# Two-input SBUF operations moved from GpSimd to VectorE, SBUF copies and 256-channel norms to ScalarE, in a streaming encoder step

## The chip, the cores and the metric

The kernel runs on one core of a Trainium2 chip. The metric is the device time of one launch in microseconds (us). The engines are PE (TensorE, matrix products), DVE (VectorE), ACT (ScalarE), POOL (GpSimd) and SP (SyncE, which issues nearly all transfers). Each takes its instructions strictly in the order of its own list and meets the others only at semaphores.

## The reference, cut to what matters

One encoder layer over 512 prompt tokens and 64 sample tokens of 1024 channels, in float32:

```python
xn = rms_norm(x, g_norm)
hq, hf, hi, za, dq, dk, dv, zb, mq, zm, gr = split_columns(xn @ w_in)   # 13312 columns
y_a = rms_norm(hgrn2_recurrence(...), g_hg_out)       # 8 heads of 128
y_b = rms_norm(diff_softmax(norm(dq), norm(dk), dv)) * (1 - lam_init)   # 8 heads, two maps of 64
y_m = memory_attention(rms_norm(mq, g_mq), mem_k, mem_v)                # 4 heads of 256, 256 memories
h = sum(sigmoid(gr[n]) * ((y_n * silu(z_n)) @ w_branch[n]) for n in range(3))
y = x + h @ w_out
```

`mem_k` and `mem_v` are projections of a normed memory (`w_mkv`); `mem_k` is normed over its 256 channels per head. The sample tokens attend to cached keys and values and carry a recurrent state.

## The kernel before, in words

Precision comes from splitting. Every float32 operand of a large product is held as a rounded high part and a remainder; a product is three matmuls (high by high, high by low, low by high). ACT writes the high part (a copy that rounds, line 214 for weights), DVE or POOL subtracts it from the source to get the low part (line 217).

Work is a list of *jobs*, each for 256 columns of a weight matrix. A job's weights come as two halves (`raw`, three buffers) and are split into *units* of 128x512 (`wh`, `wl`, eight in flight). Jobs are of three kinds. "T" gives channels by tokens (line 332, 296 for its product), "N" gives tokens by channels (line 332 and 345), and "S" is a 2x2 block product with seven instead of eight block products (`strassen`, line 416 on; matmuls on line 459). An S job needs sums of its weight blocks, t1 to t4, made in `plan` by `add` (line 248), and sums of blocks of x, made once in `build_XS` (line 374) and kept in `XS`. Its seven steps of 12 matmuls use four PSUM banks out of a ring of three; evacuations on DVE (lines 424 and 432) free them, so a late one stops PE at a later step or at the next job.

The order of all work is written by the program itself. `run_jobs` walks through the jobs; after every 12 matmuls it makes one *tick* (`weave`): it emits what was put off by `later(n, ...)`, and it advances each running generator by one step. The generators are the attention and recurrence heads; their small matmuls and transposes thus stand between the steps of the jobs. `conv_next` adds one or two weight units per tick. The engines' lists follow this order.

The stages, with their jobs and the generators beside them: the recurrence heads (`hgrn`, jobs of kind T and N); branch 0's output product, beside which `build_XS` runs; the memory's keys and values, the gates `gr` (S); the memory heads (`mem_q_prep`, `mem_kv`, `mem_head`) beside S jobs; the differential heads (`diff_pair`, finished by `finish_heads`) beside N and S jobs; branches 2 and 1 (line 296) with the merge in `branch_jobs`; the output product. `y_splits` (line 654) fetches a branch's outputs again and splits them for the branch product.

POOL has these parts in the stages after the recurrence: every second weight remainder (line 217, by `lo_engine` or by name in `plan`), t3 and t4 (line 248), the remainders of `y_splits` (line 678) and `split_slot` (line 724), half of `build_XS` (line 380), gains in the norms (line 1040), copies between partition halves in `build_k` (line 1113) and `build_s` (1142, 1143), the merge's last add for branch 2 (line 1677), and `rstd`, the power -1/2 on a few columns (lines 140 and 141). In `mem_head`, DVE scales the softmax (line 1518) before PE transposes it (line 1531); in `finish_heads`, DVE scales a head by the softmax's sum (line 739) and by the norm (line 752) before PE transposes it (line 761); in `combine`, DVE joins the two maps (line 1198) before PE transposes them (line 1209).

Of the kernel before, what the change touches and what calls it, by code (L numbers as in the profile page):

```python
# [13 lines left out]
F32 = mybir.dt.float32  # L14
# [7 lines left out]
P = 128  # L22
# [44 lines left out]
def encoder_step(ctx, tc, ins, outs):  # L67
# [101 lines left out]
    def lo_engine():  # L169
        lo_n[0] += 1  # L170
        return ge if lo_n[0] % 2 == 0 else ve
# [28 lines left out]
    def plan(i, j):  # L200
# [38 lines left out]
        else:  # L239
# [11 lines left out]
            def op_t2(now):  # L251
                t1 = add("t1", part(0, 0), part(0, 1), ve)
                t2 = add("t2", sums["t1"], part(1, 1), ve)
                sums["slots"] = t1, t2, add("t3", part(0, 1), part(1, 1), ge)
# [4 lines left out]
            def op_t1(now):  # L259
                t4 = add("t4", sums["t2"], part(1, 0), ge)  # L260
# [5 lines left out]
            ops.append((i, 0, lambda now: split(part(0, 0), P, 0, now, ge)))  # L266
            ops.append((i, 1, op_t2))
            ops.append((i, 1, op_t1))
            ops.append((i, 1, lambda now: split(part(1, 0), P, 1, now, ge)))
            ops.append((i, 1, lambda now: split(sums["t3"], P, None, now, ve, 0, sums["slots"][2])))  # L270
            ops.append((i, 1, lambda now: split(part(1, 1), P, 1, now, ge)))
            ops.append((i, 1, lambda now: split(sums["t4"], P, None, now, ge, 0, sums["t4slot"])))
# [101 lines left out]
    def build_XS():  # L374
# [7 lines left out]
        for k2 in range(2):  # L382
# [5 lines left out]
            tt(ge, t, l22, l21)  # L388
# [3 lines left out]
            tt(ge, s3, h11, h21)  # L392
            ve.scalar_tensor_tensor(out=s2, in0=s1, scalar=-1.0, in1=h11, op0=ALU.mult, op1=ALU.subtract)
            yield
            tt(ge, t, l11, l21)
            tt(ve, s2, s2, l11)
            yield
            tt(ge, s3, s3, t, ALU.add)
# [3 lines left out]
            for n, x in enumerate((s1, s2, s3, s4)):  # L402
# [3 lines left out]
                tt(ge if n % 2 else ve, lo, x, hi.bitcast(F32))  # L406
# [247 lines left out]
    def y_splits(n):  # L654
# [8 lines left out]
        for h in range(8):  # L663
# [14 lines left out]
            ge.tensor_tensor(out=lo[:, 0:TT], in0=tmp[:, 0:TT], in1=hi[:, 0:TT].bitcast(F32), op=ALU.subtract)  # L678
# [37 lines left out]
    def split_slot(x):  # L716
# [6 lines left out]
        def flo():  # L723
            ge.tensor_tensor(out=lo[:, 0:512], in0=x[:, 0:512], in1=hi[:, 0:512].bitcast(F32), op=ALU.subtract)
            slots.put(x)
# [4 lines left out]
    def finish_heads(n, ob, ons, ohp, j, gcol, z, r0=None):  # L730
# [7 lines left out]
        if r0 is not None:  # L738
            ve.tensor_tensor(out=o3, in0=ob.rearrange("p (a b) -> p a b", a=4), in1=r0.unsqueeze(2).to_broadcast([P, 4, P]), op=ALU.mult)
            src = on[:, 0:512]  # L740
            put(ob)
            yield
# [4 lines left out]
        se.activation(out=sq[0:TS, 0:P], in_=ons[0:TS], func=AF.Square, accum_out=ss[0:TS, 4:5])  # L747
        rstd(rs[:, 0:4], ss[:, 0:4], P)
        rstd(rs[0:TS, 4:5], ss[0:TS, 4:5], P)
        for _ in range(4):  # L750
            yield
        ve.tensor_tensor(out=o3, in0=src.rearrange("p (a b) -> p a b", a=4), in1=rs[:, 0:4].unsqueeze(2).to_broadcast([P, 4, P]), op=ALU.mult)
# [259 lines left out]
    def norm_groups(bufs, smp, g, gain=None):  # L1012
# [23 lines left out]
        def apply(x, r):  # L1036
            ve.tensor_tensor(out=grp(x), in0=grp(x), in1=r.unsqueeze(2).to_broadcast([x.shape[0], r.shape[1], g]), op=ALU.mult)
            if gain is not None:
                gb = gain[0 : x.shape[0]].unsqueeze(1).to_broadcast([x.shape[0], r.shape[1], g])
                ge.tensor_tensor(out=grp(x), in0=grp(x), in1=gb, op=ALU.mult)  # L1040
# [3 lines left out]
        if smp is not None:  # L1044
            apply(smp, rs[0:TS, m : m + ns])
            yield
        yield
# [887 lines left out]
```

## Time and profile before

| | us |
|---|---|
| three runs | 1149.35, 1146.55, 1148.5; median 1148.5 |
| the profiled execution, its own time | 1149.15 |
| its span, first to last instruction | 1147.4 |
| PE busy in it | 1098.0 |
| DVE, POOL, ACT busy | 818.0, 612.3, 528.5 |
| mean granted TensorE clock | 0.985 of full speed |

A row of a view by stretches gives, for each engine, busy time and the number of instructions, then the granted TensorE clock (1.00 is full speed), the busy share of the DMA engines and GB/s. A row of waits gives who waited, for whom, the total in us, how often, and the longest. A row of groups gives line, engine, operation, tiles (out<-in), shapes and number, then busy time and the mean of one in ns, then idle time of the engine just before and what ended it. A row of the timeline gives start, duration, engine and operation, and in brackets the idle time before it and what ended that. `slot` stands for any of the general buffers, `d` for a bank of the jobs' products, `abank` for a bank of the heads.

### The profile page before, as it was taken

How to read it: one execution, taken by the hardware profiler on the slowest of the kernel's cores; microseconds unless marked ns; L12 is line 12 of the kernel's file. 1: busy time of each engine (PE TensorE's matmuls, PEld its weight loads, DVE VectorE, ACT ScalarE, POOL GpSimd, SP SyncE). 2: the span in 40 equal slices, each digit the busy share in tenths (PEclk: the TensorE clock that was granted, in tenths of full speed). 3: DMA queues.
4: the chain of work that ended last, by engine and by line, in shares of the span. 5: the costliest groups of instructions: out<-in, count | busy, mean ns of one | idle time of the engine just before them, and what ended most of it. 6: DMA issues, size and time to landing. Idle time of an engine off the chain costs nothing. (4 is left out here: it accounts for less than half of the span.)

```text
span 1147.4 us, 22458 instructions
## 1 busy us (share of the span) xinstructions
PE 1098.0 (96%) x8685; PEld 1079.0 (94%) x8685; DVE 818.0 (71%) x1391; ACT 528.5 (46%) x1227; POOL 612.3 (53%) x682
## 2 busy tenths in 40 slices
PE   8999999998999999989999989998998998999998
PEld 6999999998999999989899989998998998888998
DVE  6479493956637855799895669779869877856532
ACT  6443333233233554646664446645645754543320
POOL 2336444456536876987562564366447485454120
PEclk9999999999999999999999989999999999998999
DMA  5442132234234566634434332223222437555542
GB/s 185 148 152 79 57 105 88 88 102 127 73 111 144 188 221 229 216 128 140 152 116 163 112 108 96 79 88 108 73 81 78 160 123 242 170 181 176 166 133 68
DMA packets 127931, 150.67 MB, mean 131 GB/s; under 512 B 7730, under 2 KB 104654, under 8 KB 127824
## 3 DMA queue, kind: packets, MB, share of 16 engines
q1 hardware_dynamic: 127820, 149.24, 40.5%
q8 instruction: 68, 1.11, 0.4%
q14 instruction: 39, 0.32, 0.1%
q10 hardware_dynamic: 4, 0.00, 0.0%
HBM read 114.74 MB, written 34.47 MB: 130 GB/s over the span
## 5 line engine op out<-in xcount | busy, mean ns | idle before, releaser
L217 POOL TENSOR_TENSOR wl<-raw,wh 128x512 fp32r<-128x512 f32 x172 | 252.7, 1474 | 262.9 <-ACT wh L214 256.1
L332 PE MATMUL d<-wh,xh 128*128 128x256 f32 x768 | 223.4, 291 | 0.7 <-ACT xh L621 0.7
L332 PE MATMUL d<-wh,xl 128*128 128x256 f32 x768 | 218.5, 285 | 1.3 <-DVE xl L624 1.3
L332 PE MATMUL d<-wl,xh 128*128 128x256 f32 x768 | 218.3, 284 | 0.0
L214 ACT ACTIVATE wh<-raw 128x512 fp32r<-128x512 f32 x284 | 167.8, 622 | 4.1 <-DMA raw<-in_w_in_dram 2.2
L296 PE MATMUL d<-slot,wh 128*128 128x288 f32 x768 | 160.1, 303 | 5.1 <-POOL slot L678 5.1
L332 PEld LDWEIGHTS d<-wh,xh 128*128 128x128 f32 x768 | 148.0, 193 | 1.8 <-ACT xh L621 1.1
L332 PEld LDWEIGHTS d<-wh,xl 128*128 128x128 f32 x768 | 147.9, 193 | 1.8 <-DVE xl L624 1.8
L332 PEld LDWEIGHTS d<-wl,xh 128*128 128x128 f32 x768 | 148.2, 193 | 0.4
L217 DVE TENSOR_TENSOR wl<-raw,wh 128x512 fp32r<-128x512 f32 x112 | 116.2, 1040 | 43.7 <-ACT wh L214 42.5
L296 PEld LDWEIGHTS d<-slot,wh 128*128 128x128 f32 x768 | 126.8, 193 | 6.6 <-POOL slot L678 6.2
L459 PE MATMUL d<-XS,wh 128*128 128x288 f32 x640 | 131.5, 299 | 0.0
L296 PE MATMUL d<-xh,wh 128*128 128x288 f32 x384 | 116.8, 304 | 0.0
L296 PE MATMUL d<-slot,wl 128*128 128x288 f32 x384 | 115.2, 300 | 0.0
L296 PE MATMUL d<-xh,wl 128*128 128x288 f32 x384 | 113.1, 295 | 0.0
L296 PE MATMUL d<-xl,wh 128*128 128x288 f32 x384 | 113.1, 295 | 0.0
L459 PEld LDWEIGHTS d<-XS,wh 128*128 128x128 f32 x640 | 103.0, 190 | 0.3
L459 PE MATMUL d<-XS,wl 128*128 128x288 f32 x320 | 94.6, 295 | 0.0
L217 DVE TENSOR_TENSOR wl<-slot,wh 128x512 fp32r<-128x512 f32 x60 | 82.7, 1396 | 12.3 <-ACT wh L214 11.8
L459 PE MATMUL d<-xh,wh 128*128 128x288 f32 x240 | 75.2, 313 | 8.7 <-DVE slot L424 4.4
L459 PE MATMUL d<-xh,wl 128*128 128x288 f32 x240 | 73.1, 305 | 1.9 <-POOL wl L217 1.9
L296 PEld LDWEIGHTS d<-slot,wl 128*128 128x128 f32 x384 | 74.2, 193 | 0.0
(321 smaller groups left out, 2741.5 us busy)
## 6 DMA issues: line engine op xcount, KB each, us to landing
raw<-in_w_in_dram SPq DMA_DIRECT2D x104, 512.0 KB
raw<-in_w_branch_dram SPq DMA_DIRECT2D x24, 512.0 KB
raw<-in_w_mkv_dram SPq DMA_DIRECT2D x16, 512.0 KB
out_dram<-slot SPq DMA_DIRECT2D x31, 256.0 KB
g<-slot SPq DMA_DIRECT2D x24, 288.0 KB
slot<-g SPq DMA_DIRECT2D x24, 288.0 KB
y<-slot SPq DMA_DIRECT2D x20, 288.0 KB
slot<-y SPq DMA_DIRECT2D x20, 288.0 KB
```

The source lines that it names most:

```text
L214: se.activation(out=u.hi, in_=src, func=AF.Copy)
L217: (eng or lo_engine()).tensor_tensor(out=u.lo, in0=src, in1=u.hi.bitcast(F32), op=ALU.subtract)
L296: pe.matmul(out=ps[:, 0:TH], lhsT=w[:, k % 4, :], rhs=x(k)[:, sl], start=(n == 0), stop=(n == 23))
L332: pe.matmul(out=ps[:, t * CW : (t + 1) * CW], lhsT=x(k)[:, sl], rhs=w[:, k % 2, :], start=(n == 0), stop=(n == 23))
L459: pe.matmul(out=ps, lhsT=w[:, k, :], rhs=x(k), start=bool(first and n == 0), stop=stop, skip_group_check=True)
```

## The change

From the moment `XS` exists (that is, from branch 0's output product on), no weight remainder goes to POOL. The sums t3 and t4, `build_XS`, the remainders in `y_splits` (of the first stage as well) and `split_slot`, the gains, and the merge's last add go to DVE. In `build_k` both copies between partition halves go to ACT. The scaling of the softmax in `mem_head` goes to ACT. The norms over 256 channels (memory keys, memory queries) get a function of their own, `norm_256`: one Square per row block with its sum accumulated on ACT, and the scaling on ACT too; the gain is a DVE multiplication one tick later. In `finish_heads`, for the differential heads, the PSUM bank is copied unscaled by ACT, and the softmax's factor is applied to the small columns (its square to the sums, itself to the result of `rstd`). POOL keeps `rstd`, memsets, the small copies in `build_s`, and all that it does in the recurrence stage except `y_splits`.

```diff
     def lo_engine():
         lo_n[0] += 1
-        return ge if lo_n[0] % 2 == 0 else ve
+        return ge if lo_n[0] % 2 == 0 and not XS else ve
...
-                sums["slots"] = t1, t2, add("t3", part(0, 1), part(1, 1), ge)
+                sums["slots"] = t1, t2, add("t3", part(0, 1), part(1, 1), ve)
...
-                t4 = add("t4", sums["t2"], part(1, 0), ge)
+                t4 = add("t4", sums["t2"], part(1, 0), ve)
...
-            ops.append((i, 0, lambda now: split(part(0, 0), P, 0, now, ge)))
+            ops.append((i, 0, lambda now: split(part(0, 0), P, 0, now, ve)))
...
-            ops.append((i, 1, lambda now: split(part(1, 0), P, 1, now, ge)))
+            ops.append((i, 1, lambda now: split(part(1, 0), P, 1, now, ve)))
...
-            ops.append((i, 1, lambda now: split(part(1, 1), P, 1, now, ge)))
-            ops.append((i, 1, lambda now: split(sums["t4"], P, None, now, ge, 0, sums["t4slot"])))
+            ops.append((i, 1, lambda now: split(part(1, 1), P, 1, now, ve)))
+            ops.append((i, 1, lambda now: split(sums["t4"], P, None, now, ve, 0, sums["t4slot"])))
...
             tt(ve, s1, h22, h21)
-            tt(ge, t, l22, l21)
+            tt(ve, t, l22, l21)
...
-                tt(ge if n % 2 else ve, lo, x, hi.bitcast(F32))
+                tt(ve, lo, x, hi.bitcast(F32))
...
-            ge.tensor_tensor(out=lo[:, 0:TT], in0=tmp[:, 0:TT], in1=hi[:, 0:TT].bitcast(F32), op=ALU.subtract)
+            ve.tensor_tensor(out=lo[:, 0:TT], in0=tmp[:, 0:TT], in1=hi[:, 0:TT].bitcast(F32), op=ALU.subtract)
...
         if r0 is not None:
-            ve.tensor_tensor(out=o3, in0=ob.rearrange("p (a b) -> p a b", a=4), in1=r0.unsqueeze(2).to_broadcast([P, 4, P]), op=ALU.mult)
+            se.activation(out=on[:, 0:512], in_=ob, func=AF.Copy)
             src = on[:, 0:512]
+            r2 = small(4, "r2", bufs=3)
+            ve.tensor_tensor(out=r2, in0=r0, in1=r0, op=ALU.mult)
...
+        if r0 is not None:
+            ve.tensor_tensor(out=ss[:, 0:4], in0=ss[:, 0:4], in1=r2, op=ALU.mult)
...
+        if r0 is not None:
+            ve.tensor_tensor(out=rs[:, 0:4], in0=rs[:, 0:4], in1=r0, op=ALU.mult)
...
+    def norm_256(bufs, smp=None, gain=None):
+
+        rows = [(b[:, 256 * t : 256 * t + 256], P) for b in bufs for t in range(2)] + ([(smp, TS)] if smp is not None else [])
...
+        for i, (x, r) in enumerate(rows):
+            se.activation(out=sq[0:r, 0:256], in_=x, func=AF.Square, accum_out=ss[0:r, i : i + 1])
+            if i % 2:
+                yield
...
+        rstd(rs[:, 0:m], ss[:, 0:m], 256)
...
+        for _ in range(4):
+            yield
+        for i, (x, r) in enumerate(rows):
+            se.activation(out=x, in_=x, func=AF.Copy, scale=rs[0:r, i : i + 1])
+            if gain is not None:
+                later(1, lambda x=x: ve.tensor_tensor(out=x, in0=x, in1=gain, op=ALU.mult))
+            if i % 2:
+                yield
...
                 ve.tensor_tensor(out=KL[m][a, 0:T], in0=ps[a], in1=KD[m][a, 0:T].bitcast(F32), op=ALU.subtract)
-                ve.tensor_copy(KD[m][b, 0:T], KD[m][a, 0:T].bitcast(F32))
-                ge.tensor_copy(KL[m][b, 0:T], KL[m][a, 0:T].bitcast(F32))
+                se.activation(out=KD[m][b, 0:T], in_=KD[m][a, 0:T].bitcast(F32), func=AF.Copy)
+                se.activation(out=KL[m][b, 0:T], in_=KL[m][a, 0:T].bitcast(F32), func=AF.Copy)
...
             ve.reciprocal(out=zz[0:R], in_=zz[0:R])
-            ve.tensor_scalar(out=e[0:R, 0:256], in0=e[0:R, 0:256], scalar1=zz[0:R], scalar2=None, op0=ALU.mult)
+            se.activation(out=e[0:R, 0:256], in_=e[0:R, 0:256], func=AF.Copy, scale=zz[0:R])
...
-                (ve if n == 1 else ge).tensor_tensor(out=h2[b][:, sl], in0=h2[b][:, sl], in1=g[:, sl], op=ALU.add)
+                ve.tensor_tensor(out=h2[b][:, sl], in0=h2[b][:, sl], in1=g[:, sl], op=ALU.add)
```

Over the whole program DVE's list grows from 1370 rows to 1578, ACT's from 1084 to 1164, and POOL's shrinks from 685 to 410. Because `norm_256` takes two ticks less than the norm that it replaces for the memory queries, the memory heads' transposes and small products stand up to two ticks earlier between the same matmuls of the jobs, and a few of their transfers stand some rows earlier in SP's list.

The first place is the list of DVE in an S job beside the first memory head, at the end of one job's steps: lines 248 and 217 make t1, t2 and the remainders of the next job, line 424 and 432 evacuate this one. Before:

```order
L424 TENSOR_TENSOR slot_194_4972<-d_6302,slot_194_4972 128x288
L248 TENSOR_TENSOR slot_249_6336<-raw_6168 128x512
L248 TENSOR_TENSOR slot_250_6338<-slot_249_6336,raw_6189 128x512
L217 TENSOR_TENSOR wl_6343<-slot_250_6338,wh_6342 128x512
L217 TENSOR_TENSOR wl_6361<-slot_249_6336,wh_6360 128x512
L424 TENSOR_TENSOR slot_195_4973<-d_6302,slot_194_4972 128x288
L432 SCALAR_TENSOR_TENSOR slot_254_6385<-slot_196_4974,slot_195_4973 128x288
```

The list of POOL for the same stretch holds this before:

```order
L217 TENSOR_TENSOR wl_6296<-slot_238_6184,wh_6295 128x512
L217 TENSOR_TENSOR wl_6316<-raw_6168,wh_6315 128x512
L248 TENSOR_TENSOR slot_251_6340<-raw_6168,raw_6189 128x512
L248 TENSOR_TENSOR slot_252_6358<-slot_250_6338,raw_6189 128x512
L217 TENSOR_TENSOR wl_6382<-raw_6189,wh_6381 128x512
```

DVE's list for the same stretch in the changed kernel (its lines 218, 249, 425 and 433 are lines 217, 248, 424 and 432 of before):

```order
L425 TENSOR_TENSOR slot_194_4973<-d_6307,slot_194_4973 128x288
L218 TENSOR_TENSOR wl_6321<-raw_6176,wh_6320 128x512
L249 TENSOR_TENSOR slot_247_6341<-raw_6176 128x512
L249 TENSOR_TENSOR slot_248_6343<-slot_247_6341,raw_6197 128x512
L249 TENSOR_TENSOR slot_249_6345<-raw_6176,raw_6197 128x512
L249 TENSOR_TENSOR slot_250_6363<-slot_248_6343,raw_6197 128x512
L218 TENSOR_TENSOR wl_6348<-slot_248_6343,wh_6347 128x512
L218 TENSOR_TENSOR wl_6366<-slot_247_6341,wh_6365 128x512
L425 TENSOR_TENSOR slot_195_4974<-d_6307,slot_194_4973 128x288
L433 SCALAR_TENSOR_TENSOR slot_252_6392<-slot_196_4975,slot_195_4974 128x288
```

The two evacuations (line 424 before, 425 now) had four rows of DVE between them, with POOL's rows beside those; now seven rows stand between them, all on DVE, and POOL's list has none of the five.

The second place is ACT's list in `build_k`, at the start of a differential head: line 1091 writes the queries' high parts, 1108 the keys', 439 evacuates a job, 214 splits weights. Before:

```order
L1091 ACTIVATE slot_413_8699<-abank_81,gdq 64x512
L1091 ACTIVATE slot_414_8700<-abank_81,gdq 64x512
L1108 ACTIVATE slot_415_8730<-abank_84 64x512
L1108 ACTIVATE slot_416_8731<-abank_84 64x512
L439 ACTIVATE slot_196_4974<-d_8738 128x288
L214 ACTIVATE wh_8757<-slot_420_8753 128x512
L214 ACTIVATE wh_8796<-slot_419_8751 128x512
```

In the changed kernel (lines 1125, 1142, 440, 215 are the same code, 1146 and 1147 the two copies that DVE and POOL had):

```order
L1142 ACTIVATE slot_407_8734<-abank_84 64x512
L1142 ACTIVATE slot_408_8735<-abank_84 64x512
L440 ACTIVATE slot_196_4975<-d_8742 128x288
L215 ACTIVATE wh_8761<-slot_412_8757 128x512
L215 ACTIVATE wh_8800<-slot_411_8755 128x512
L1146 ACTIVATE slot_407_8734<-slot_407_8734 64x512
L1147 ACTIVATE slot_409_8736<-slot_409_8736 64x512
L1170 ACTIVATE slot_414_8780<-abank_83 64x320
L1171 ACTIVATE slot_414_8780<-abank_83,gdq 64x64
```

Two copies have come into ACT's list; the second (line 1147) reads what DVE's subtraction of the same tick writes, and the first transposed samples (line 1170) and the later weight splits stand behind it.

More of the change, by code (lines that the diff above doesn't have):

```diff
@@ L391, in build_XS @@
             yield
-            tt(ge, s3, h11, h21)
+            tt(ve, s3, h11, h21)
             ve.scalar_tensor_tensor(out=s2, in0=s1, scalar=-1.0, in1=h11, op0=ALU.mult, op1=ALU.subtract)
             yield
-            tt(ge, t, l11, l21)
+            tt(ve, t, l11, l21)
             tt(ve, s2, s2, l11)
             yield
-            tt(ge, s3, s3, t, ALU.add)
+            tt(ve, s3, s3, t, ALU.add)
             ve.scalar_tensor_tensor(out=s4, in0=s2, scalar=-1.0, in1=h12, op0=ALU.mult, op1=ALU.subtract)
@@ L723, in flo @@
         def flo():
-            ge.tensor_tensor(out=lo[:, 0:512], in0=x[:, 0:512], in1=hi[:, 0:512].bitcast(F32), op=ALU.subtract)
+            ve.tensor_tensor(out=lo[:, 0:512], in0=x[:, 0:512], in1=hi[:, 0:512].bitcast(F32), op=ALU.subtract)
             slots.put(x)
@@ L1039, in apply @@
                 gb = gain[0 : x.shape[0]].unsqueeze(1).to_broadcast([x.shape[0], r.shape[1], g])
-                ge.tensor_tensor(out=grp(x), in0=grp(x), in1=gb, op=ALU.mult)
+                ve.tensor_tensor(out=grp(x), in0=grp(x), in1=gb, op=ALU.mult)
         for i, b in enumerate(bufs):
@@ L1046, in norm_groups @@
             yield
+        yield
+        yield
+    def norm_256(bufs, smp=None, gain=None):
+        rows = [(b[:, 256 * t : 256 * t + 256], P) for b in bufs for t in range(2)] + ([(smp, TS)] if smp is not None else [])
+        ss = small(5, "ssn256", bufs=3)
+        rs = small(5, "rsn256", bufs=3)
+        sq = slots.get()
+        for i, (x, r) in enumerate(rows):
+            se.activation(out=sq[0:r, 0:256], in_=x, func=AF.Square, accum_out=ss[0:r, i : i + 1])
+            if i % 2:
+                yield
+        slots.put(sq)
+        yield
+        m = 2 * len(bufs)
+        rstd(rs[:, 0:m], ss[:, 0:m], 256)
+        if smp is not None:
+            rstd(rs[0:TS, m : m + 1], ss[0:TS, m : m + 1], 256)
+        for _ in range(4):
+            yield
+        for i, (x, r) in enumerate(rows):
[3 more added lines that the diff above has]
+            if i % 2:
+                yield
         yield
@@ L1357, in mem_k_prep @@
     def mem_k_prep(h, mk):
-        yield from norm_groups([mk], None, 256, gain=gmk[0][:, 0:256])
+        yield from norm_256([mk], gain=gmk[0][:, 0:256])
         if h == 3:
@@ L1434, in mem_q_prep @@
         sy.dma_start(out=ck[:, 0:512].rearrange("p (t c) -> p t c", t=2), in_=I["cache_mem_k"][0, 0].rearrange("(t p) h c -> p t h c", p=P)[:, :, h, :])
-        yield from norm_groups([A["q", 0], A["q", 1]], A["qs"][0:TS], 256)
+        yield from norm_256([A["q", 0], A["q", 1]], A["qs"][0:TS])
         yield
```

## The prediction

> **What bounds the kernel now.** I read three views in this order: stretches, the waits of PE, the timeline at the longest wait. First the stretches of 100 us from 350 us on, where the change acts (the first column of busy time is PE, then weight loads, DVE, ACT, POOL, then the granted clock):
>
> ```profile
> 350.00:450.00 100.00, 99.26 (x774) 98.79 (x773) 72.27 (x68) 49.40 (x99) 80.36 (x56) 1.00 0.56 184
> 450.00:550.00 100.00, 91.38 (x693) 89.95 (x692) 85.05 (x103) 53.92 (x116) 77.35 (x61) 0.98 0.53 170
> 550.00:650.00 100.00, 98.64 (x753) 96.10 (x751) 74.14 (x131) 51.74 (x123) 48.15 (x42) 1.00 0.44 140
> 650.00:750.00 100.00, 96.59 (x740) 95.08 (x738) 80.69 (x161) 58.81 (x150) 53.55 (x54) 0.97 0.33 104
> 750.00:850.00 100.00, 94.16 (x742) 92.24 (x741) 83.24 (x155) 57.87 (x141) 53.62 (x57) 0.98 0.27 84
> 850.00:950.00 100.00, 94.37 (x750) 93.13 (x751) 79.31 (x150) 58.74 (x143) 66.83 (x62) 0.98 0.36 115
> 950.00:1050.00 100.00, 89.28 (x622) 86.13 (x622) 75.15 (x147) 45.99 (x113) 53.93 (x62) 0.93 0.60 202
> sum 700.00, PE 663.69 PEld 651.41 DVE 549.86 ACT 376.48 POOL 433.80; mean PE 94.81 PEld 93.06 DVE 78.55 ACT 53.78 POOL 61.97
> ```
>
> PE is busy nearly always, and the change takes no product from it. What can be won is PE's idle time, 700 - 663.7 = 36.3 us, and what the clock loses: the shares missing from 1.00 make 2 + 3 + 2 + 2 + 7 = 16 us (rounded to whole us per stretch). Together some 52 us of a profiled execution of 1149.15 us. Who ends PE's idle time in these 700 us:
>
> ```profile
> PE abank L1531 <- DVE slot L1518: 6.7, 5, 3.0
> PE abank L761 <- DVE slot L752: 5.4, 4, 3.5
> PE d L296 <- POOL slot L678: 5.1, 4, 2.4
> PE d L459 <- DVE slot L424: 4.4, 2, 4.0
> PE d L459 <- DVE slot L693: 4.3, 2, 2.6
> PE abank L1170 <- DVE slot L1112: 2.6, 1, 2.6
> PE abank L1209 <- DVE slot L739: 2.2, 1, 2.2
> PE abank L1209 <- DVE slot L1198: 1.9, 4, 0.7
> PE d L459 <- POOL wl L217: 1.9, 2, 1.1
> PE abank L1394 <- DMA slot<-memk: 0.8, 1, 0.8
> PE abank L1081 <- ACT slot L1186: 0.7, 2, 0.4
> ```
>
> The first nine, 34.5 us, name DVE or POOL; a transfer and ACT come last. The longest wait shows why they are late. These are rows of DVE, POOL and PE there:
>
> ```profile
> 498.23 7.24 DVE L217 TENSOR_TENSOR wl<-slot,wh 128x512 fp32r<-128x512 f32 x2 [0.76 <-ACT wh L214]
> ...
> 498.12 1.28 POOL L217 TENSOR_TENSOR wl<-slot,wh 128x512 fp32r<-128x512 f32 x1
> 499.37 1.28 POOL L217 TENSOR_TENSOR wl<-raw,wh 128x512 fp32r<-128x512 f32 x1
> 500.61 1.27 POOL L248 TENSOR_TENSOR slot<-raw,raw 128x512 f32<-128x512 f32 x1
> 501.85 1.26 POOL L248 TENSOR_TENSOR slot<-slot,raw 128x512 f32<-128x512 f32 x1
> 503.07 1.26 POOL L217 TENSOR_TENSOR wl<-raw,wh 128x512 fp32r<-128x512 f32 x1
> ...
> 505.90 0.61 PE L459 MATMUL d<-xh,wh 128*128 128x288 f32 x1 [4.01 <-DVE slot L424]
> ```
>
> Two subtractions hold DVE for 7.24 us while POOL runs five of its own without a pause; PE waits 4.01 us for the evacuation behind them. With POOL idle the same pair is another thing (a row of DVE, and the stretch around it, in which POOL is 0.00):
>
> ```profile
> 558.71 1.28 DVE L217 TENSOR_TENSOR wl<-slot,wh 128x512 fp32r<-128x512 f32 x2
> ...
> 558.70:560.00 1.30, 1.30 (x12) 1.30 (x11) 1.30 (x4) 0.46 (x2) 0.00 (x0) 1.00 0.96 310
> ```
>
> 1.28 us for two, so 0.60 for each further one and 0.68 for the last: POOL takes 1.26 to 1.28 for one, and DVE gets nothing done beside it when both operands of its operation lie in SBUF. The two engines work these operations off in turn, and POOL's share is the slow one. The Trainium skill says the same in "SBUF — State Buffer", section "Who interferes with whom": a VectorE instruction with two SBUF inputs and a GpSimd one that reads SBUF exclude each other for the whole of an instruction. The trace goes further than that sentence: DVE was shut out over several of POOL's instructions, not one.
>
> **The moved operations.** How much DVE is given, in the same 700 us (busy time and number, DVE's then POOL's; the first row is line 217, the second line 248):
>
> ```profile
> 350.00:1050.00 700.00, 143.57 (x115) 198.78 (x136) 0.98 0.44 143
> 350.00:1050.00 700.00, 44.93 (x40) 57.43 (x40) 0.98 0.44 143
> ```
>
> DVE's own 155 of these took 188.5 us; free of POOL they take 155 x 0.605 = 94 us, so 94 us of blocking go. POOL's 176 come over at 0.605 each, 106 us. The rest of the moved work is in DVE's list: 1578 - 1370 = 208 rows more, net of those that go to ACT, so some 208 x 0.605 = 126 us in all if each were of the large size. DVE then needs about 549.9 - 94 + 126 = 582 us, while PE's own work is 700 - 36.3 - 16 = 648 us: 90%, an upper estimate, since the blocking of lines 1037, 1198 and 380 goes too and is not counted. No engine is full on average; a single burst is what matters.
>
> I take the nine waits in four groups.
>
> (a) Behind the blocked pair, and behind POOL itself: lines 678, 424, 693 and 217, 5.1 + 4.4 + 4.3 + 1.9 = 15.7 us. In the place shown, five POOL operations and two of DVE are worked off in 7.24 us; seven on DVE take 7 x 0.605 = 4.2 us, 3.0 us less. DVE also comes to them earlier, since its earlier bursts are shorter. Of the 4.01 us of PE some 0.4 to 1.0 remain. I take nine tenths of the group, 14.1 us; the ends are 11.8 (three quarters, by the burst alone) and 15.7. What hides the moved work here are the two steps between an evacuation and the next use of its bank, 24 matmuls, which is 3.2 us at PE's pace there (three matmuls in 0.40 us); work beyond that is uncovered.
>
> (b) The softmax of the memory heads (line 1531 for 1518), 6.7 us. Its scaling leaves DVE's list, but the reciprocal ahead of it stays there, and ACT now waits for that. Rows ahead of it lose their blocking, and gain one or two moved rows of 0.605. Half, 3.4 us; between 0 and 6.7.
>
> (c) The differential heads (lines 752, 739, 1198), 5.4 + 2.2 + 1.9 = 9.5 us. At the 2.2 us wait this stood on DVE:
>
> ```profile
> 998.21 1.31 DVE L1198 SCALAR_TENSOR_TENSOR slot<-slot,cc 128x128 f32<-128x128 f32 x1
> 999.45 0.68 DVE L739 TENSOR_TENSOR slot<-abank,rz 128x512 f32<-128x512 f32 x1
> ```
>
> 1.31 us for 128 columns is blocking once more, and line 739 goes to ACT; against it stand a weight remainder and the merge's add, both moved here. A third, 3.2 us; between -3 and 9.5.
>
> (d) Line 1170 behind 1112, 2.6 us. DVE's cast goes to ACT, into the middle of the same chain. Nothing, between -3 and 2.6.
>
> Together 20.7 us of PE's idle time. The clock follows the waits: 16 us for 36.3 us of idle time is 0.44 for each, so 9.1 us more.
>
> One rule on the clock has to be weighed here. The wait for line 1112, and the stretch after it:
>
> ```profile
> 961.91 0.30 PE L1170 MATMUL abank<-slot,slot 128*128 128x128 f32 x1 [2.65 <-DVE slot L1112]
> ...
> 963.00:966.00 3.00, 3.00 (x15) 2.96 (x14) 2.88 (x8) 0.46 (x2) 2.06 (x4) 0.50 0.42 129
> ```
>
> After 2.65 us of idle time the clock was 0.50 for the next 3 us. So waits well short of the longest already cost clock, and I let the clock come back only in proportion. The Trainium skill has it otherwise: "TensorE: Matmul & The Clock Gate", section "What's actually happening", puts the drop to half after an idle window of about 3.4 us. By that rule no wait left after the change would cost clock, all 16 us would come back, and the sum below would be about 1115, inside the forecast's own range; the trace does not agree with the rule, at 2.65 us.
>
> **What it adds on ACT.** ACT goes from 1084 to 1164 rows and is busy 58.8 us in 100 at most (650 to 750, 850 to 950); the copies of `build_k`, the norms and the scalings fit. They bring waits, though: ACT stands still until DVE has got to the reciprocal (20 times) and to line 1111's subtraction (16 times), and behind it stand weight splits and evacuations. What such a wait took of POOL, in line 1113 before (a row of groups):
>
> ```profile
> L1113 POOL CAST slot<-slot 64x512 fp32r<-64x512 f32 x16 | 12.5, 784 | 28.7 <-DVE slot L1111 26.9 <-issue 1.5
> ```
>
> At most 26.9 us move into ACT's list from there, and at least nothing reaches PE, since ACT has 40 us free in 100. Of the nine rows none names ACT, and the row that does has 0.7 us. I take 3 us; a gain is excluded, since these are added waits. Freeing POOL makes `rstd` come sooner, which no wait of PE asked for: nothing. `build_XS` goes from two engines to one, 24 operations with PE at 99.26 of 100 beside it: nothing. The tick shifts of the memory heads move small matmuls and their transfers between the same steps: nothing, and 2 us either way in the range.
>
> The sum: 1149.15 - 20.7 - 9.1 + 3 = 1122.4, so **1122 us**. The profiled execution lies 0.65 us above the median of 1148.5; that is less than the last digit of my terms.
>
> **The rivals.**
>
> *All waits go.* If every burst of DVE fits under its cover, all 36.3 us and the 16 us go: 1149.15 - 52.3 = 1097, with 3 us on ACT 1100. For it: none of the nine waits is on a transfer or on ACT. Against it: DVE at up to 90%. Chance 0.15.
>
> *DVE is full where it matters.* In 450 to 550 DVE is at 85.05 with PE at 91.38. If the burst on DVE stays as long as the blocked one (because the rows that it waits for come in late), each wait stays as it is: 1149, no change. The Trainium skill names the other way of sharing in "Perfetto Trace Analysis", section "Optimizing Scalar/DVE Operations": work of a saturated VectorE may go to ScalarE or even GpSimd, which this change undoes; the 7.24 us row speaks against that here. Chance 0.10.
>
> *ACT waits in DVE's place.* The mechanism: in `build_k` ACT stops at line 1147 until DVE has done its subtraction, with weight splits and an evacuation behind it, so PE lacks weights or a bank. The price: 26.9 us in 11 waits is 2.45 each, for 16 of them 39 us, with 0.44 of clock 56 us; against it the gain of 29.8. If all of it reaches PE: 1149.15 - 29.8 + 56 = 1175. It decides from about half of it on. For it: ACT's list is strict, and each of the eight heads has two such copies. Against it: ACT's free 40 us in 100, and that PE lost to ACT less than to any of the nine rows. Chance 0.11.
>
> That the change doesn't do what it says is excluded by the lists: POOL's has 275 rows fewer, and none of line 248.
>
> **How the numbers follow.** The forecast has 0.64, the rivals 0.15, 0.10 and 0.11. About 0.3%, 3.4 us, is what a measurement here can tell from no change. Forecast and full gain are faster, and a little of the second rival; so faster 0.80, same 0.08, slower 0.12. The low end is the full gain, 1100. The high end is the forecast with the lower ends of (a) to (d), 2.3 + 3.4 + 6.2 + 3 = 14.9 us less with their clock of 6.6, which gives 1144; no change and the slower rival, 0.2 together, lie beyond it.
>
> **What would show it.** Right: DVE's line 217 at about 0.6 us everywhere after 350 us, no row of it above 2 us; the waits for lines 424, 693, 678 and 217 nearly gone; the clock at 1.00 in 450 to 550 and higher than 0.93 near the end. Line 1209 and line 761 still wait for DVE. Wrong: PE waiting for ACT (lines 214, 439 or 1147's successor), a DVE above 95% in any 100 us, or PE's idle time unchanged with a DVE that is no longer blocked.

## The result and the profile after

| | us |
|---|---|
| before, four runs in the same rounds | 1148.82 (1146.55 to 1149.35) |
| changed, four runs | 1121.55 (1120.05 to 1122.42) |
| ratio | 0.9753, 95% interval 0.973 to 0.9775 |
| the changed kernel's profiled execution, its own time | 1122.42 |

The changed kernel is faster by 27.3 us of the medians; the forecast was 1122. The page of the changed kernel's profile, with the busy totals and, by 40 slices, POOL and the granted clock:

```profile
PE 1091.1 (97%) x8685; PEld 1073.7 (96%) x8685; DVE 789.9 (70%) x1603; ACT 573.3 (51%) x1355; POOL 233.4 (21%) x406
...
POOL 2435455453610000000000210140221131010000
PEclk9999999999999999999999999999999999999999
```

POOL is busy for less than a tenth of each slice from the 13th, where `XS` exists, to the 22nd, and for at most four tenths after that. DVE has 212 instructions more than before (1603 against 1391) and is nevertheless busy for a shorter time, 789.9 us against 818.0. The two slices with a clock below 9 tenths that the page of before had are gone. The stretches of 100 us in the changed kernel, columns as in the prediction:

```profile
350.00:450.00 100.00, 100.00 (x783) 100.00 (x782) 68.44 (x116) 53.48 (x115) 2.66 (x6) 1.00 0.60 195
450.00:550.00 100.00, 99.87 (x770) 99.19 (x769) 79.82 (x150) 70.02 (x169) 5.90 (x13) 1.00 0.57 181
550.00:650.00 100.00, 100.00 (x776) 98.33 (x775) 63.07 (x132) 59.44 (x152) 13.29 (x18) 1.00 0.41 132
650.00:750.00 100.00, 99.00 (x781) 97.50 (x780) 81.69 (x189) 66.52 (x163) 16.19 (x25) 1.00 0.32 102
750.00:850.00 100.00, 96.11 (x755) 94.90 (x754) 80.59 (x186) 64.19 (x154) 19.02 (x29) 0.98 0.29 89
850.00:950.00 100.00, 94.66 (x736) 92.87 (x735) 84.22 (x201) 71.01 (x170) 19.59 (x31) 0.98 0.48 163
950.00:1050.00 100.00, 92.79 (x668) 89.76 (x667) 72.34 (x167) 45.60 (x109) 6.58 (x13) 0.97 0.54 181
sum 700.00, PE 682.43 PEld 672.54 DVE 530.16 ACT 430.25 POOL 83.24; mean PE 97.49 PEld 96.08 DVE 75.74 ACT 61.47 POOL 11.89
```

PE's idle time is 700 - 682.4 = 17.6 us, where it was 36.3. The clock loses 2 + 2 + 3 = 7 us, where it lost 16. These two, 18.7 + 9, are 27.7 us, and the profiled executions differ by 1149.15 - 1122.42 = 26.7: the whole gain lies here. Between 350 and 650 us almost none of these two losses is left; what remains is nearly all in the last three stretches. The waits of PE in the changed kernel:

```profile
PE d L297 <- DVE slot L679: 3.5, 4, 1.1
PE d L460 <- ACT slot L440: 2.9, 2, 1.9
PE abank L768 <- DVE slot L759: 2.1, 3, 1.0
PE abank L1204 <- ACT slot L1146: 2.1, 1, 2.1
PE abank L1276 <- ACT slot L1246: 1.8, 1, 1.8
PE abank L1115 <- ACT slot L1220: 1.8, 2, 1.0
PE abank L1205 <- ACT slot L1147: 1.1, 1, 1.1
PE d L460 <- DVE slot L694: 0.9, 1, 0.9
PE abank L1243 <- DVE r L743: 0.8, 1, 0.8
```

(Line 679 is line 678 of before, 694 is 693, 440 is 439, 759 is 752, 1220 is 1186; 1146 and 1147 are the copies that `build_k` gave to ACT.) The long rows are gone: softmax, line 424 and POOL's own. A new kind has come: five rows name ACT, 2.9 + 2.1 + 1.8 + 1.8 + 1.1 = 9.7 us, where ACT stood for 0.7.

The same place as in the prediction's longest wait, on DVE in the changed kernel:

```profile
491.92 0.69 DVE L249 TENSOR_TENSOR slot<-raw 128x512 f32<-128x512 f32 x1
492.64 0.69 DVE L249 TENSOR_TENSOR slot<-slot,raw 128x512 f32<-128x512 f32 x1
493.25 0.69 DVE L249 TENSOR_TENSOR slot<-raw,raw 128x512 f32<-128x512 f32 x1
493.85 0.68 DVE L249 TENSOR_TENSOR slot<-slot,raw 128x512 f32<-128x512 f32 x1
494.45 1.29 DVE L218 TENSOR_TENSOR wl<-slot,wh 128x512 fp32r<-128x512 f32 x2
...
496.14 0.46 DVE L433 SCALAR_TENSOR_TENSOR slot<-slot,slot 128x288 f32<-128x288 f32 x1
```

Four sums and two remainders, with no POOL instruction beside them, are done in 3.8 us (491.92 to 495.74); before, the two remainders by themselves took 7.24. All remainders of that form over the whole program (instructions, then shortest, median and longest in ns):

```profile
L218 DVE TENSOR_TENSOR wl<-slot,wh x80: 673/683/694, 388.6 to 856.6; 128x512 fp32r<-128x512 f32 x80
```

Eighty instructions lie within 21 ns of each other. There is no blocked one left, and after 350 us no instruction of DVE takes more than 1.5 us. Before 350 us, where POOL keeps its share of the remainders, one on DVE still takes 4.40 us (at 88.75 us).

### The profile page after: what moved, and what is told of

Its sections match the earlier page's. It is cut to its first block, busy times and chain, and to the rows that moved or that the text cites. A ratio compares the mean times of both kernels' runs of the same rounds, so it can differ in the third digit from the quotient of the medians.

```text
span 1120.7 us, 22273 instructions
## 1 busy us (share of the span) xinstructions
PE 1091.1 (97%) x8685; PEld 1073.7 (96%) x8685; DVE 789.9 (70%) x1603; ACT 573.3 (51%) x1355; POOL 233.4 (21%) x406
## 4 chain that ended last, share of the span: by engine, by line
PE 81%; DVE 9%; DMA 3%; ACT 3%; issue 2%; POOL 1%; SPq 1%; DVEq 0%; ACTq 0%; POOLq 0%
PE d L297 26%; PE d L333 25%; PE d L460 14%; PE d L346 4%; DVE wl L218 3%; PE abank L1276 1%; DMA raw<-in_w_in_dram 1%; PE abank L1530 1%; DVE slot L249 1%; PE abank L1243 1%; PE abank L912 1%; PE abank L1597 1%; PE abank L1205 1%; ACT wh L215 1%; PE abank L948 1%
## 5 line engine op out<-in xcount | busy, mean ns | idle before, releaser
L218 DVE TENSOR_TENSOR wl<-raw,wh 128x512 fp32r<-128x512 f32 x240 | 171.8, 732 | 54.2 <-ACT wh L215 52.8
L297 PE MATMUL d<-xh,wh 128*128 128x288 f32 x384 | 116.7, 304 | 0.0
L297 PE MATMUL d<-xh,wl 128*128 128x288 f32 x384 | 113.1, 294 | 0.0
L218 POOL TENSOR_TENSOR wl<-raw,wh 128x512 fp32r<-128x512 f32 x44 | 64.4, 1467 | 70.3 <-ACT wh L215 70.3
L460 PE MATMUL d<-xh,wh 128*128 128x288 f32 x240 | 72.7, 303 | 3.9 <-ACT slot L440 2.9
L140 POOL TENSOR_SCALAR rsn<-ssn 128x16 f32<-128x16 f32 (+4 forms) x28 | 7.4, 264 | 329.0 <-ACT slot L1064 250.8
L297 PEld LDWEIGHTS d<-xh,wh 128*128 128x128 f32 x384 | 72.1, 188 | 0.5
```

What stands on the lines that cost most here:

```text
L218: (eng or lo_engine()).tensor_tensor(out=u.lo, in0=src, in1=u.hi.bitcast(F32), op=ALU.subtract)
L297: pe.matmul(out=ps[:, 0:TH], lhsT=w[:, k % 4, :], rhs=x(k)[:, sl], start=(n == 0), stop=(n == 23))
L460: pe.matmul(out=ps, lhsT=w[:, k, :], rhs=x(k), start=bool(first and n == 0), stop=stop, skip_group_check=True)
```

## The experiments

Theory 1 is the prediction's: DVE's operations with two SBUF inputs and POOL's reads of SBUF take turns, DVE's bursts got long by that, and the gain comes from taking POOL's large reads away. Theory 2 is the rival that the relief of DVE by ACT (scalings, norms, copies) brings the gain. The times are medians with the lowest and highest run; ratios are to the kernel before in the same rounds, with the 95% interval. Where a kernel has useless work on POOL, its results are read by nobody.

**The moves alone.** All that went to ACT is put back; the moves from POOL to DVE stay.

```diff
-                se.activation(out=KD[m][b, 0:T], in_=KD[m][a, 0:T].bitcast(F32), func=AF.Copy)
-                se.activation(out=KL[m][b, 0:T], in_=KL[m][a, 0:T].bitcast(F32), func=AF.Copy)
+                ve.tensor_copy(KD[m][b, 0:T], KD[m][a, 0:T].bitcast(F32))
+                ge.tensor_copy(KL[m][b, 0:T], KL[m][a, 0:T].bitcast(F32))
...
-        yield from norm_256([mk], gain=gmk[0][:, 0:256])
+        yield from norm_groups([mk], None, 256, gain=gmk[0][:, 0:256])
...
-            se.activation(out=e[0:R, 0:256], in_=e[0:R, 0:256], func=AF.Copy, scale=zz[0:R])
+            ve.tensor_scalar(out=e[0:R, 0:256], in0=e[0:R, 0:256], scalar1=zz[0:R], scalar2=None, op0=ALU.mult)
```

(and `finish_heads` and the norm of the memory queries likewise)

> The changed kernel with everything that went to ScalarE put back where it was (256-channel norms, the softmax scaling, the scaling of the differential heads and one copy of build_k on VectorE, the other copy of build_k on GpSimd); only the two-input SBUF operations stay moved from GpSimd to VectorE. Theory 1, turn-taking (a GpSimd operation that reads SBUF shuts out a VectorE one with two SBUF inputs, and VectorE does the same work in half the time): the waits of group (a) go, 1149 - 14.1 - 6.2 of clock = about 1129, at least 1135. Theory 2, relief (VectorE's list gets shorter by what ScalarE takes, and that is what lets PE go): VectorE's list only gets longer here, so no gain, 1149 or more. VectorE's line 217/218 rows at 0.6 to 0.7 us by theory 1.

1115.84 us (1115.14 to 1117.38), ratio 0.9717 (0.9696 to 0.9739). The moves by themselves give the whole gain and some us more, and 13 us more than theory 1 had forecast from group (a) alone. The fullest stretch for DVE in this kernel, and then its waits of PE:

```profile
450.00:550.00 100.00, 99.90 (x774) 99.51 (x773) 89.86 (x174) 62.76 (x137) 8.71 (x13) 1.00 0.55 180
```

```profile
PE d L297 <- DVE slot L679: 3.7, 4, 1.3
PE abank L1198 <- DVE slot L1140: 3.1, 1, 3.1
PE abank L1109 <- ACT slot L1214: 2.9, 4, 1.1
PE d L460 <- DVE slot L425: 1.5, 2, 0.7
PE abank L762 <- DVE slot L753: 1.5, 2, 0.9
PE abank L1237 <- DVE slot L740: 1.3, 1, 1.3
PE d L460 <- DVE slot L694: 1.1, 2, 0.8
```

DVE at 89.86 of 100 leaves PE at 99.90: a full DVE hurts nobody as long as no single burst is long. No row names the softmax, though its scaling is back on DVE.

**ACT's part alone.** The kernel before, with the scalings, norms and copies on ACT, and POOL keeping its sums, remainders and gains.

```diff
-                ve.tensor_copy(KD[m][b, 0:T], KD[m][a, 0:T].bitcast(F32))
-                ge.tensor_copy(KL[m][b, 0:T], KL[m][a, 0:T].bitcast(F32))
+                se.activation(out=KD[m][b, 0:T], in_=KD[m][a, 0:T].bitcast(F32), func=AF.Copy)
+                se.activation(out=KL[m][b, 0:T], in_=KL[m][a, 0:T].bitcast(F32), func=AF.Copy)
...
-            ve.tensor_scalar(out=e[0:R, 0:256], in0=e[0:R, 0:256], scalar1=zz[0:R], scalar2=None, op0=ALU.mult)
+            se.activation(out=e[0:R, 0:256], in_=e[0:R, 0:256], func=AF.Copy, scale=zz[0:R])
```

(and `norm_256` and `finish_heads` as in the change)

> The kernel before with only what went to ScalarE (256-channel norms, softmax scaling, scaling of the differential heads, both copies of build_k); all two-input SBUF operations stay on GpSimd where they were. Theory 1, turn-taking: line 217 on VectorE stays at 1.1 to 1.4 us on average with rows of several us; group (b) may go, 6.7 us and its clock of 3, so 1139 to 1149. Theory 2, relief: most of the gain, 1122 to 1130.

1152.34 us (1149.99 to 1154.96), ratio 1.0032 (1.0017 to 1.0047): no gain, and a little beyond what theory 1 allowed. Theory 2 falls. Its remainders on DVE, and then its waits of PE:

```profile
L217 DVE TENSOR_TENSOR wl<-slot,wh x60: 674/910/6466, 387.8 to 869.7; 128x512 fp32r<-128x512 f32 x60
```

```profile
PE abank L767 <- DVE slot L758: 8.5, 4, 5.5
...
PE abank L1564 <- ACT slot L1551: 2.0, 1, 2.0
```

One remainder still takes 6.47 us. The softmax wait (line 1564 here, 1531 before) fell from 6.7 to 2.0 us, but the wait for line 758 (752 before) went from 5.4 to 8.5 us: the blocking shows at another row instead.

**The weights alone.** The kernel before, with only t3, t4 and the weights' remainders moved (no `build_XS`, `y_splits`, gains or merge).

```diff
-        return ge if lo_n[0] % 2 == 0 else ve
+        return ge if lo_n[0] % 2 == 0 and not XS else ve
...
-                t4 = add("t4", sums["t2"], part(1, 0), ge)
+                t4 = add("t4", sums["t2"], part(1, 0), ve)
...
-            ops.append((i, 0, lambda now: split(part(0, 0), P, 0, now, ge)))
+            ops.append((i, 0, lambda now: split(part(0, 0), P, 0, now, ve)))
```

> The kernel before with only the weight remainders (after the recurrence) and the weight sums t3 and t4 on VectorE, 176 of GpSimd's operations; XS, the branch outputs' remainders, gains, the merge and all ScalarE parts as before. Theory 1, turn-taking: most of group (a) without line 678 goes, 10.6 us and 4.7 of clock, so 1130 to 1138. Theory 2, relief: nothing was taken off VectorE, so 1149 or more.

1122.66 us (1119.42 to 1124.84), ratio 0.9772 (0.9745 to 0.98). This is 26 us, more than theory 1 gave it; all moves together gave 33 us in the same rounds, so some 7 us come from the others. What it leaves of PE's waits, two of the rows:

```profile
PE d L296 <- POOL slot L678: 5.4, 5, 2.4
...
PE abank L761 <- DVE slot L752: 2.1, 3, 1.0
```

The wait for POOL's line 678 stands, since `y_splits` was not moved. Line 752 is down from 5.4 to 2.1 us, and no row names line 1518, though neither was touched: the blocking of the heads' and the softmax's rows came from the weights' work too.

**Useless reads put back on POOL.** The changed kernel, and twelve additions of a small constant tile to itself on POOL in each job with sums.

```diff
+    idle = cst.tile([P, P], F32, name="idle")
...
+                for _ in range(12):
+                    ge.tensor_tensor(out=idle, in0=ident, in1=ident, op=ALU.add)
```

> The changed kernel, with useless work on GpSimd: at each of the 20 block jobs, 12 additions of 128x128 with both inputs in SBUF, into a tile that nobody reads. No wait hangs on them except GpSimd's own rstd behind them. Theory 1, turn-taking: while they run VectorE's line 218 is shut out, rows of 2 us and more come back, PE waits for lines 425 and 694 again; 1132 to 1150. Theory 3 (GpSimd was only a slow producer, 1.3 us where VectorE takes 0.6, and PE waited for its results; shutting out plays no part): nobody waits for these results, so 1119 to 1125, at most a little more by rstd.

1129.1 us (1126.04 to 1132.63), ratio 0.9827 (0.9805 to 0.985). This costs 7.6 us (6.1 against the next run, of the same rounds). It lies between the two theories, above the 1125 of theory 3 and below the 1132 of theory 1. The additions, and the remainders beside them, as groups:

```profile
L255 POOL TENSOR_TENSOR idle<-ident 128x128 f32<-128x128 f32 x228 | 141.6, 621 | 17.0
L219 DVE TENSOR_TENSOR wl<-raw,wh 128x512 fp32r<-128x512 f32 x176 | 123.8, 721 | 18.0 <-ACT wh L216 17.6
```

Short operations of POOL lengthened DVE's remainders only from 685 to 721 ns on the mean; the shortest of the additions took 391 ns and their mean 621, so here it is rather POOL that loses.

**Useless writes instead.** Twenty-four memsets of the same tile in the place of the twelve additions.

```diff
+                for _ in range(24):
+                    ge.memset(idle, 0.0)
```

> The counterpart: the same with 24 memsets of the same tile in place of the 12 additions, about as long on GpSimd (0.2 us each by the profile of before, 4.8 us per job), which write SBUF but read none of it. It holds the wait of rstd behind useless work the same. Theory 1, turn-taking over reads: 1119 to 1125, VectorE's line 218 at 0.6 to 0.7 us. If the useless work acts through rstd's delay or through writes alone, it is as slow as the run with additions.

1122.96 us (1120.94 to 1124.84), ratio 0.9773 (0.9755 to 0.979). The memsets and the remainders, as groups:

```profile
L255 POOL MEMSET idle<- 128x128 f32 x456 | 93.4, 205 | 25.6
L219 DVE TENSOR_TENSOR wl<-raw,wh 128x512 fp32r<-128x512 f32 x178 | 119.1, 685 | 18.7 <-ACT wh L216 17.9
```

93 us of writes on POOL leave the remainders at 685 ns and the time at 1.4 us above the changed kernel's. So it is reading that costs, and not POOL's being busy. `rstd`, which stands behind this work in POOL's list, could be held up by 24 x 0.205 = 4.9 us in a job, and that cost next to nothing. The Trainium skill says this of the pair in "SBUF — State Buffer", section "Who interferes with whom": a VectorE instruction with two SBUF inputs contends with a GpSimd instruction that reads SBUF, not with one that only writes; the 205 ns and 685 ns agree.

**Wider reads, each waiting for the one before.** Six additions of 384 columns per job, all into one tile.

```diff
+    idle = cst.tile([P, 3 * P], mybir.dt.bfloat16, name="idle")
+    wide = ident.unsqueeze(1).to_broadcast([P, 3, P])
...
+                for _ in range(6):
+                    ge.tensor_tensor(out=idle.rearrange("p (a b) -> p a b", b=P), in0=wide, in1=wide, op=ALU.add)
```

> The additions of 128x128 on GpSimd cost 8 us and left no VectorE row of line 217's kind above 2 us: short operations lost the turn as often as they took it. Here the useless work has nearly the size of the work that was moved: six additions of 128x384 per block job (two inputs in SBUF, a bf16 output that nobody reads), some 1 us each. Theory 1, turn-taking, in the form that GpSimd's next long operation is ready before VectorE gets its turn: VectorE rows above 2 us come back, 1132 to 1150. If the length plays no part, 1126 to 1132 as with the short ones.

1147.66 us (1142.03 to 1150.57), ratio 0.9987 (0.9968 to 1.0007): the whole gain is taken back by work that nobody needs, so theory 3 (POOL merely a slow producer) falls. PE's idle time between 350 and 1050 us is 35.2 us and the clock loses 16, as in the kernel before (36.3 and 16). Rows of DVE in this kernel beside a burst of these additions (its lines 220, 251 and 429 are 218, 249 and 425 of the changed kernel):

```profile
497.53 1.31 DVE L251 TENSOR_TENSOR slot<-raw 128x512 f32<-128x512 f32 x1
...
502.47 2.54 DVE L220 TENSOR_TENSOR wl<-slot,wh 128x512 fp32r<-128x512 f32 x2
```

The same six instructions that took 3.8 us take 7.5 (497.53 to 505.01), each one about 1.25 us instead of 0.6. A late `rstd` is not the reason: no wait of PE names POOL, and DVE and ACT together wait 4.5 + 1.7 = 6.2 us for it in the 700 us, against 2.4 + 2.1 = 4.5 with the memsets. But no single one was shut out for several of POOL's, as it was before the change: that part of the expectation was missed. Each addition here waits for the one before (one output tile), with about 78 ns between them, and DVE gets every other turn.

**Narrower reads without a gap.** Twelve additions of 192 columns per job, into two tiles in turn, so that none waits for the one before.

```diff
+    idle = [cst.tile([P, 192], mybir.dt.bfloat16, name=f"idle{i}") for i in range(2)]
+    wide = ident[:, 0 : P // 2].unsqueeze(1).to_broadcast([P, 3, P // 2])
...
+                for n in range(12):
+                    ge.tensor_tensor(out=idle[n % 2].rearrange("p (a b) -> p a b", b=P // 2), in0=wide, in1=wide, op=ALU.add)
```

> Of the wide additions each waits for the one before (they write one tile), which leaves 60 to 80 ns between two on GpSimd, and VectorE got its turn in these gaps: no row above 2 us, though the time was that of the kernel before. Here useless work of about the same length (12 additions of 128x192 per block job) writes two tiles in turn, so that the next one is ready when one ends, as the moved work of the kernel before was. If the gap is what lets VectorE in, rows of VectorE above 2 us come back and the time is 1145 to 1165. If VectorE gets every second turn anyhow, no row above 2 us, and 1129 (short ones) to 1148 (long ones).

1166.82 us (1165.87 to 1168.84), ratio 1.0156 (1.0127 to 1.0184), a little above the 1145 to 1165 that was expected. DVE, POOL and PE at its longest wait, one timeline each:

```profile
528.55 1.91 DVE L220 TENSOR_TENSOR wl<-slot,wh 128x512 fp32r<-128x512 f32 x2
530.38 0.41 DVE L1542 TENSOR_REDUCE mx<-abank 128x1 f32<-128x256 f32 x1
530.71 0.44 DVE L429 TENSOR_TENSOR slot<-d,slot 128x288 f32<-128x288 f32 x1
531.19 13.40 DVE L437 SCALAR_TENSOR_TENSOR slot<-slot,slot 128x288 f32<-128x288 f32 x1
```

```profile
528.95 15.31 POOL L256 TENSOR_TENSOR idle<-ident 128x192 bf16<-128x192 f32 x31
```

```profile
545.61 0.85 PE L464 MATMUL d<-XS,wh 128*128 128x288 f32 x2 [9.79 <-DVE slot L437]
```

The instruction that takes 0.46 us in the changed kernel (its line 433) took 13.40 us, until POOL's list of additions ended, and PE stood still for 9.79 us behind it. The additions of three jobs ran in one piece there, since POOL had stood for 21.23 us until ACT had done what the next `rstd` needed. The long blocking is back, and it needs POOL without a gap: the additions with gaps were shorter (128 columns) and longer (384) than these, and neither kind brought it.

The absent gap is not enough, though. Beside the first of these same additions, from 524.90 to 530.46 us, four sums and two remainders of DVE stood back to back and took 0.88 to 0.99 us each: there both engines got every other turn. The blocked instruction came after two that read a PSUM bank (lines 1542 and 429). Each of the six DVE instructions above 1.5 us after 350 us in this kernel came right after one that reads PSUM or has one input only. In the 7.24 us row of before, DVE came to POOL's burst after 0.76 us of idle time; there the first subtraction took 6.64 us, the second 0.68. So in most rows two engines that both had their next instruction ready alternated, and DVE was shut out where it came to a burst of POOL already running without a gap. One row of before does not fit (a remainder of 4.91 us at 779.12 us, straight behind the two-input line 752), and no run tests this by itself: what decides the turn stays open.

**Where some us are lost on ACT.** The moves alone had come out below the changed kernel. The expectations name their theories anew for each kernel: theory A puts the loss into the differential heads, first into `build_k`, theory B into the memory heads or the finish. Three kernels put parts of ACT's work back, and both kernels were run again.

```diff
-                se.activation(out=KD[m][b, 0:T], in_=KD[m][a, 0:T].bitcast(F32), func=AF.Copy)
-                se.activation(out=KL[m][b, 0:T], in_=KL[m][a, 0:T].bitcast(F32), func=AF.Copy)
+                ve.tensor_copy(KD[m][b, 0:T], KD[m][a, 0:T].bitcast(F32))
+                ge.tensor_copy(KL[m][b, 0:T], KL[m][a, 0:T].bitcast(F32))
```

> The changed kernel with the two copies of build_k back on VectorE (high part) and GpSimd (low part); all else as changed. Theory A (the loss of 6 us against the run with the moves alone is ScalarE's in build_k: it stops at line 1147, and evacuations, line 440, and the samples' transposed halves, line 1170, come late): 1121.5 - 3.2 of the waits for 1146 and 1147 - up to 2.9 of those for line 440, with 0.44 of clock, so 1113 to 1118. Theory B (the loss is from the memory heads and the finish, whose scalings now wait for VectorE's reciprocal in ScalarE's list): 1120 to 1123.

1119.35 us (1115.77 to 1123.49), ratio 0.974 (0.9716 to 0.9764): between the two, inconclusive. Next the memory heads' part put back on DVE (the norm of the memory queries likewise):

```diff
-        yield from norm_256([mk], gain=gmk[0][:, 0:256])
+        yield from norm_groups([mk], None, 256, gain=gmk[0][:, 0:256])
...
-            se.activation(out=e[0:R, 0:256], in_=e[0:R, 0:256], func=AF.Copy, scale=zz[0:R])
+            ve.tensor_scalar(out=e[0:R, 0:256], in0=e[0:R, 0:256], scalar1=zz[0:R], scalar2=None, op0=ALU.mult)
```

> The changed kernel with the norms over 256 channels and the softmax scaling of the memory heads back on VectorE; build_k and the differential heads' finish as changed. Theory A (the loss is build_k's): 1120 to 1123, and group (b), the wait of line 1531's transposes, stays near zero since turn-taking made it. Theory B: 1114 to 1118. If the parts on ScalarE were what removed group (b), it comes back here with up to 6.7 us and its clock, 1124 to 1131.

1121.23 us (1117.34 to 1125.57), ratio 0.976 (0.9734 to 0.9786): it changes nothing, neither gain nor loss, as theory A has it. Then the reverse, only the memory heads' part on ACT, with `build_k` and `finish_heads` as before (the rest of `finish_heads` and `build_k` as in the moves alone):

```diff
-            se.activation(out=on[:, 0:512], in_=ob, func=AF.Copy)
+            ve.tensor_tensor(out=o3, in0=ob.rearrange("p (a b) -> p a b", a=4), in1=r0.unsqueeze(2).to_broadcast([P, 4, P]), op=ALU.mult)
```

> The moves, and of the parts on ScalarE only those of the memory heads (256-channel norms, softmax scaling); build_k and the differential heads' finish are as before. Theory A (the loss is in the differential heads, ScalarE holding evacuations back behind line 1147): as fast as the moves alone, 1114 to 1118. Theory B (the loss is in the memory heads): as slow as the changed kernel, 1119 to 1123.

1117.3 us (1115.43 to 1118.34), ratio 0.9717 (0.9693 to 0.974). Together with it ran the changed kernel again,

> The changed kernel itself once more, on one chip with the next two, since the single runs of one kernel lie up to 8 us apart and the comparisons of a few us between kernels came from different chips. 1119 to 1123 by every theory.

1121.56 us (1118.65 to 1124.55), ratio 0.9753 (0.9728 to 0.9779), and the moves alone again,

> The moves alone once more beside the changed kernel. If the parts on ScalarE cost time, 3 to 7 us below the changed kernel in the same rounds (1114 to 1118); if the earlier difference was the chip's or chance, within 2 us of it.

1119.08 us (1115.78 to 1121.47), ratio 0.9732 (0.9707 to 0.9757): 2.5 us below the changed kernel, between the two expectations. Over all runs the changed kernel stands at a mean of 1121.4 (nine runs), the moves alone at 1117.7 (nine), the memory heads' part on ACT at 1117.2 (six). So ACT's work in the differential heads, `build_k` and `finish_heads` together, costs about 4 us, and the versions without it are the fastest; the intervals of single comparisons overlap. Which of the two it is stays open. With `build_k`'s copies off ACT (the first of the three kernels) the PE waits for line 440 and for line 1246 are gone, which points to `build_k`, but that kernel's times spread over 7.7 us.

## Why the prediction was right, point by point

**The mechanism** was right and is shown: moves without ACT give all of the gain, ACT without moves none, useless reads on POOL take it back, useless writes don't. Both rivals that saw the burst on DVE stay long or ACT take over fall by the result; *all waits go* was too much by the 17.6 us of idle time and the 7 us of clock that remain. One part of the mechanism was incomplete: the engines do not simply take turns. The long rows were DVE shut out over a whole burst of POOL, and only some rows show turns.

**The sum.** Forecast 29.8 us of gain less 3 of new waits. Measured by the same terms:

| term | forecast | measured |
|---|---|---|
| (a) lines 678, 424, 693, 217 | -14.1 | 15.7 to 4.4: -11.3 |
| (b) softmax | -3.4 | 6.7 to 0: -6.7 |
| (c) differential heads | -3.2 | 9.5 to 2.9: -6.6 |
| (d) line 1170, now for ACT | 0 | 2.6 to 3.2: +0.6 |
| new waits for ACT elsewhere | +3 | 0.7 to 6.5: +5.8 |
| clock | -9.1 | -9 |

The waits come to -18.2 against -17.7, and the clock is as forecast. That the total is closer than its terms is luck: misses of both signs cancel.

- (a) lies below its low end of 11.8. What remains is line 297 waiting for 679, 3.5 of 5.1 us: `y_splits` came to DVE, which does one remainder in 0.75 us where POOL took 1.43 (medians), yet behind other rows of its own list. "Nine tenths" had no row behind it for this part.
- (b) and (c) were too small. The step that failed is the discount for moved rows and for ACT's new wait ("half", "a third"). Lost blocking alone was worth more than that: the softmax wait stays away where its scaling is back on DVE, and moving only the weights removes it too.
- ACT: "3 us" is too little by the names of the waits, which make 9.7 us with (d), but about right by experiment: the changed kernel is 3.7 us above the moves alone on the mean, clock included. Names mislead here, since in the moves alone most of these waits stand too: 3.1 us of line 1198 for DVE in place of the 3.2 us of lines 1204 and 1205, and 2.9 us of line 1109 for ACT in place of the 1.8 us of line 1115. Only the 2.9 us for line 440 and the 1.8 us for line 1246 are gone there. The list of ACT in the changed kernel around a PE wait of 1.89 us for line 440, and the wait:

```profile
769.50 0.63 ACT L1147 ACTIVATE slot<-slot 64x512 fp32r<-64x512 f32 x1 [0.87 <-DVE slot L1145]
770.15 0.44 ACT L693 ACTIVATE slot<-slot 128x288 f32<-128x288 f32 x1
770.61 0.43 ACT L1170 ACTIVATE slot<-abank 64x320 fp32r<-64x320 f32 x1
...
772.04 0.41 ACT L440 ACTIVATE slot<-d 128x288 f32<-128x288 f32 x1
...
772.51 0.40 PE L460 MATMUL d<-xh,wh 128*128 128x288 f32 x1 [1.89 <-ACT slot L440]
```

This is the third rival's place, and a sign that the prediction had named for being wrong, at a small price: a wait of 0.87 us for DVE's subtraction, then five short instructions ahead of the evacuation at 772.04. The prediction's argument that ACT has 40 us free in 100 is of the mean, and the same kind of argument that it had rejected for DVE.

- DVE's load was to be 582 us at most; it is 530. Lines 218 and 249 together (lines 217 and 248 before) took 171.0 + 52.7 = 223.7 us for 338 instructions, 0.66 each rather than 0.605. The rest of DVE's work fell from 549.9 - 143.6 - 44.9 = 361.4 to 306.5: the blocking of other rows, which the forecast had left out, and what went to ACT.
- The clock came back about in proportion, not in full. The trace has the loss in pieces of 3.41 us at half clock, each worth 1.7 us: nine of them in these 700 us before, four in the changed kernel. In the 3.41 us ahead of each of the four, PE stood idle for 1.89, 2.20, 1.82 and 1.52 us, so waits of less than 2 us can still cost one. After two waits of PE in the changed kernel (timeline, then the stretch behind them):

```profile
935.33 0.33 PE L1204 MATMUL abank<-slot,slot 128*128 128x128 f32 x1 [2.09 <-ACT slot L1146]
936.72 0.33 PE L1205 MATMUL abank<-slot,slot 128*128 128x128 f32 x1 [1.06 <-ACT slot L1147]
```

```profile
937.80:940.80 3.00, 2.88 (x13) 2.68 (x13) 2.88 (x7) 1.09 (x3) 0.34 (x1) 0.50 0.72 233
```

Idle pieces of 2.09 and 1.06 us, close together, are followed by a clock of 0.50. The rule of the Trainium skill that the prediction weighed (in "TensorE: Matmul & The Clock Gate", section "What's actually happening", an idle window of about 3.4 us) does not describe these either, if it is read as 3.4 us without work.

## What to carry to other kernels

Where an instruction of DVE with two SBUF inputs shows many times its usual duration, look at what POOL reads beside it: moving POOL's work onto DVE can shorten DVE's total, as 212 more instructions did here with 28 us less busy time. Judge an engine by its longest burst against the cover behind it, not by its share: DVE at 90% cost PE nothing, ACT at 64% cost it a wait. And when one change fixes a shared cause, cost all groups of waits by that cause before giving credit to the edits nearest to each.

## What the runs showed of the hardware that was not expected

- The shut-out has no bound of one instruction. It lasted as long as POOL had its next reading instruction ready: 13.40 us beside some 30 additions. A gap of about 78 ns between POOL's instructions was enough to give DVE every other turn, with no row above 2.54 us for two. Without a gap, six DVE instructions that stood back to back still got every other turn (0.88 to 0.99 us each).
- It works both ways: with short additions of POOL, POOL's own mean went to 621 ns where the shortest took 391, and DVE's remainders lost only 36 ns.
- 93 us of POOL's memsets in the same places changed no duration on DVE (685 ns with and without).
